# Encoder layer with Strassen products: VectorE takes all subtracts of Down's resident operands, earlier, and block 1's weights' sums are spread

## The chip, the core and the metric

One core of a Trainium2 chip runs the whole kernel as one program. TensorE (PE) multiplies, VectorE (DVE), ScalarE (ACT) and GpSimd (POOL) do everything elementwise, and SyncE (SP) issues the DMAs. The metric is the time of one execution on the device, in microseconds; the times given are medians of several executions.

## The reference

The kernel computes one encoder layer for two batches, 2048 and 1024 positions of width 1024, in float32. The change lies wholly in the second half, the channel mixer:

```python
def _rmsnorm(x, g):
    xf = x.astype(jnp.float32)
    y = xf * lax.rsqrt(jnp.mean(xf * xf, axis=-1, keepdims=True) + EPS)
    return (y * g.astype(jnp.float32)).astype(x.dtype)

def _channel_mixer(h, w_up, conv_w, conv_b, w_down):
    a = h @ w_up                                   # (tokens, 1024) x (1024, 5632)
    ap = jnp.pad(a, ((0, 0), (1, 1), (0, 0)))
    a = ap[:, :-2] * conv_w[0] + ap[:, 1:-1] * conv_w[1] + ap[:, 2:] * conv_w[2] + conv_b
    gate, up = a[..., :D_FF], a[..., D_FF:]        # D_FF = 2816
    return (jax.nn.gelu(gate) * up) @ w_down       # (tokens, 2816) x (2816, 1024)

def _trunk(x, ...):
    m = _token_mixer(_rmsnorm(x, pre_mix_norm[l]), ...)
    x = x + _rmsnorm(m, post_mix_norm[l])
    c = _channel_mixer(_rmsnorm(x, pre_ffn_norm[l]), ...)
    x = x + _rmsnorm(c, post_ffn_norm[l])
```

## The kernel before

**Arithmetic.** Each float32 operand is split in two parts that TensorE multiplies: `h`, a rounded copy made by a ScalarE cast, and `l = x - h`, made by a subtract on VectorE or, for some, on GpSimd. A product is then three matmuls per 128 rows of the inner dimension: h times h, h times l, l times h. On top of this each matrix product of 2x2 blocks is done in the Strassen-Winograd form: seven block products in place of eight, of sums of blocks.

**The two projections.** *Up* (h times w_up) runs in three blocks of 1024 tokens (block 0 to 2), each 22 steps. The right operands of a block, seven operands of four parts (`sox`), stay in SBUF for all its steps; the left operands, seven a step, come from the weights (`a0u` to `a6u` are loaded, then cast and subtracted into `w0u` to `w6u`). A step is seven products `p0u` to `p6u` of 12 matmuls each. Its results are combined by VectorE in PSUM (`vu`, `ru`, `p5u`, ...), go through the convolution's taps (VectorE, line 1153) and the gate: gelu on ScalarE, then GpSimd multiplies 128 x 1024 (`t0u`, line 1190). *Down* multiplies that with w_down in three groups of the inner dimension, q0 (three parts an operand, 9 matmuls a product), q1 and q2 (four parts, 12 matmuls), each 12 steps over the tokens. The resident operands of a group (`sow`, from the loaded `srw`) are 7 x 3 or 7 x 4 tiles of one unit. Here GpSimd forms the four left sums of a step (`s0d` to `s3d`, lines 181 to 184), and VectorE adds the products to the results (`c0d`, `c1d`, ..., line 1307), which wait in DRAM between groups.

**The sums of Down's weights.** Four of the seven right operands of Down are sums of blocks of w_down. They are formed once, while Up's block 1 runs: eleven times `wd_load` (four loads of 256 KB), `wd_sums` (four GpSimd operations 128 x 512, lines 126 to 128 and 694) and `wd_store` (four stores to `wo_d`).

**What sets the order.** `at(slot, order, fn)` enters a function in a table. At the end the table is run through by slot, and within a slot by order (LOAD, PREP, MM, OUT, STORE). Each engine executes its own instructions in that order, and waits by semaphores for the others. A slot holds one product of TensorE in the phases here, a step seven slots. Left operands are prepared three slots ahead of their product in blocks 1 and 2, two in Down. A change from one block or group to the next is `turnover(s, stage, order, lead, span)` (line 251): the 28 parts of the next seven operands are entered from `lead` slots ahead of the first product on, spread over `span` slots; each is loaded three slots before it is cast and subtracted (`Stage.prep`, line 148).

**Storage.** Tiles of 128 x 1024 come from a pool of 43 units, halves of 128 x 512 from a pool of 14, banks of PSUM from eight. A new tile takes the place of an old one once its last reader is done.

Of the kernel before, what the change touches and what calls it, by code (L numbers as in the profile page):

```python
# [15 lines left out]
ALU = mybir.AluOpType  # L16
# [17 lines left out]
def tile_trunk(  # L34
# [6 lines left out]
    nc = tc.nc  # L41
# [5 lines left out]
    def unit(name, dt=F32, shape=(128, 1024)):  # L47
        return U.tile(list(shape), dt, tag="u", name=name)

    def half(name, dt=F32, shape=(128, 512)):  # L50
        return H.tile(list(shape), dt, tag="h", name=name)
# [30 lines left out]
    vec = nc.vector  # L82
# [32 lines left out]
    LOAD, PREP, MM, OUT, STORE = range(5)  # L115

    def at(slot, order, fn, *args):
        events[slot].append((order, len(events[slot]), fn, args))
# [3 lines left out]
    B11, B21, T4, T2, T3, T1, B22 = range(7)  # L122

    def right_sums(t1, b11, b12, b21, b22, last=True):

        nc.gpsimd.tensor_tensor(t1, b12, b11, op=ALU.subtract)
        nc.gpsimd.tensor_tensor(b12, b22, b12, op=ALU.subtract)
        nc.gpsimd.tensor_tensor(b11, b12, b11, op=ALU.add)
        if last:
            nc.gpsimd.tensor_tensor(b21, b11, b21, op=ALU.subtract)  # L130


    class Stage:
# [14 lines left out]
        def prep(self, j, ks=range(4)):  # L148
            for k in ks:
                if k >= self.n:  # L150
                    return
                r = self.raw[j][k]
                t = unit(f"so{self.name}{j}{k}", F32R, (128, 2, 512))
                nc.scalar.copy(t[:, 0], r)
                eng = vec if k % 2 == 0 or self.name == 'x0' and j in (B11, T2) else nc.gpsimd
                eng.tensor_tensor(t[:, 1], r, t[:, 0].bitcast(F32), op=ALU.subtract)  # L156
                self.raw[j][k] = None
                self.op[j] = (self.op[j] or []) + [t]
# [74 lines left out]
    def place(s, step, which=None):  # L233

        step.s0, step.by = (s, 1) if which is None else (s + which, 2)

    def pos(step, k):
        return step.s0 + min(k, 0) + step.by * min(max(k, 0), 6) + max(k - 6, 0)

    def steps(step, ahead=2):  # L240
        at(pos(step, -6), LOAD, step.load)
        at(pos(step, -ahead), PREP - 0.2, step.sums)
        products(step)

    def products(step):
        for i, j in enumerate(step.ORDER):
            at(pos(step, i) - step.LEAD, PREP, step.prep, j)
            at(pos(step, i), MM, step.mm, j)
            at(pos(step, i), OUT, step.post, j)

    def turnover(s, stage, order=tuple(range(7)), lead=6, span=10):

        for n in range(28):
            j, k = order[n // 4], n % 4
            d = s - lead + n * span // 28
            if k % 2 == 0:
                at(d - 3, LOAD, stage.load, j, (k,))
            at(d, PREP + 0.1, stage.prep, j, (k,))
# [329 lines left out]
    for pr in range(12):  # L588
        s = SB + 7 * pr
# [97 lines left out]
            nc.sync.dma_start(bs[q], wd[(ka, kb)[q // 2], :, c : c + 512])  # L687
        raws["wd", i] = bs

    def wd_sums(i):  # L690
        t1 = half(f"wt{i}")
        bs = raws["wd", i]
        right_sums(t1, *bs, False)
        nc.gpsimd.tensor_tensor(bs[2], bs[2], bs[0], op=ALU.subtract)
        bs.append(t1)

    def wd_store(i):
        b11, b12, b21, _, t1 = raws.pop(("wd", i))
# [322 lines left out]
    for i, m in enumerate(mixes):  # L1021
        s = B1 + 4 * i
# [180 lines left out]
    s = B1 + 4 * len(mixes)  # L1203
    for blk in range(3):

        def x_src(j, a, m, dst, blk=blk):
            nc.sync.dma_start(dst[:, :m], xo_d[blk, j, :, a : a + m])

        stage = Stage(f"x{blk}", 4, x_src)
        if blk == 1:  # L1210
            for i in range(NFT // 2):
                at(s + 7 * i + 22, LOAD, wd_load, i)
                at(s + 7 * i + 25, PREP, wd_sums, i)
                at(s + 7 * i + 29, STORE, wd_store, i)
        if blk:
            turnover(s, stage, Up.ORDER, 12, 22)
        else:
            for i, j in enumerate(Up.ORDER):
                d = s + max(2 * i - 3, -2)
                at(d - 1 - (i > 0), LOAD, stage.load, j)  # L1220
                at(d, PREP - 0.3, stage.prep, j)
        for ft in range(NFT):
            u = Up(stage, blk, ft)

            pair = ft < 2 or ft > NFT - 3
            place(s - 7 * (ft % 2) if pair else s, u, ft % 2 if pair else None)
            first = blk == 0 and ft < 2
            if first:
                u.POOL = ()
                at(u.s0 - 2, LOAD, u.load)  # L1230
                at(u.s0 - 2, PREP - 0.2, u.sums)
                products(u)
            elif blk == 0:
                steps(u, 3)
            else:
                for i, j in enumerate(u.ORDER):
                    at(pos(u, i) - 6, LOAD, u.load_left, j)
                products(u)
            if blk == 0:
                at(u.s0 + (4 if pair else 2), STORE, u.sstore)  # L1240
            at(pos(u, 4), OUT + 0.1, u.centre, 1)
            at(pos(u, 4) + 1, OUT + 0.2, u.taps, 1, 0)
            at(pos(u, 4) + 2, OUT + 0.2, u.taps, 1, 1)
            at(pos(u, 6), OUT + 0.1, u.centre, 0)
            at(pos(u, 7), OUT + 0.2, u.taps, 0, 0)
            at(pos(u, 8), OUT + 0.6, u.taps, 0, 1)
            at(pos(u, 10), OUT + 0.3, u.gate)
            at(pos(u, 12), STORE, u.store)
            s += 7
        if blk == 1:  # L1250
            at(s + 5, OUT + 0.5, last_token)
            at(s + 6, STORE, last_token_store)
# [106 lines left out]
    for q in range(3):  # L1359

        def w_src(j, a, m, dst, q=q):
            k0, n = GROUPS[q]
            kk = KPAIRS.index((k0, k0 + n)) + a
            if j in (B11, B21, B22):
                k = k0 + a + (0 if j == B11 else n)
                c = 512 if j == B22 else 0
                src = wd[k : k + m, :, c : c + 512]
            else:
                src = wo_d[(T1, T2, T3, T4).index(j), kk : kk + m]
            nc.sync.dma_start(dst[:, :m], src.rearrange("k p n -> p k n"))  # L1370

        stage = Stage(f"w{q}", GROUPS[q][1], w_src)
        turnover(s, stage, Down.ORDER, *(() if q else (10, 14)))
        if q == 2:
            at(s - 2, LOAD, po_load)
        for tp in range(12):
            d = Down(stage, q, tp)
            place(s, d)
            steps(d, 3)
            if q == 0:  # L1380
                at(s + 8, STORE, d.cstore)
                s += 7
                continue
            at(s - 2, LOAD, d.cload)
            if q == 1:
                at(s + 8, STORE, d.cstore2, 0)
                at(s + 8, STORE, d.cstore2, 1)
            elif tp == 11:
                at(s + 1, LOAD, d.closing_load)
                at(s + 2, OUT + 0.1, d.square, 0, 0)  # L1390
                at(s + 4, OUT + 0.1, d.square, 1, 1)
                at(s + 5, OUT + 0.1, d.square, 0, 1)
                at(s + 6, OUT + 0.1, d.square, 1, 0)
                at(s + 6, OUT + 0.2, d.closing_out)
            else:
                e = 3 if d.closing else 0
                at(s + 10 - e, MM, d.squares)
                at(s + 11 - e, LOAD, d.xload)
                at(s + 11 - e, PREP + 0.5, d.scale)
                at(s + 12 - e, PREP + 0.5, d.yout, 1)  # L1400
                at(s + 14 - e, OUT + 0.3, d.yout, 0)
                at(s + 14 - e, STORE, d.ystore, 1)
                at(s + 15 - e, STORE, d.ystore, 0)
            s += 7
# [121 lines left out]
```

## Time and profile before

| | before |
|---|---|
| median of 3 runs | 2758.53 us (2756.62 to 2758.92) |
| the profiled execution | 2759.55 us |
| its span in the trace | 2757.6 us |
| granted TensorE clock, mean | 0.986 |
| TensorE busy | 2650.9 us, 96% |
| VectorE busy | 2156.4 us, 78% |
| ScalarE busy | 1199.7 us, 44% |
| GpSimd busy | 1172.1 us, 43% |

The span is the time from the first to the last instruction in the trace; it is a little less than the time of the execution. Busy is the sum over an engine's instructions. Since TensorE is busy nearly throughout, the interesting part is the rest of its span: where it waits, and for whom. The page's list of costly groups is a sum over all stages and doesn't tell this; the table of stretches and the timelines do. Matmul records are pipelined and their ends modelled, so a count of matmuls in a stretch says more than the busy time.

### The profile page before, as it was taken

Reading aid. Unit: us, or ns where it says so; the run is one execution under the profiler, and the core shown is the slowest. Engines: PE = TensorE matmul, PEld = TensorE weight load, DVE = VectorE, ACT = ScalarE, POOL = GpSimd, SP = SyncE. Lnnn points to the kernel's source line nnn. Section 1 sums busy time; section 2 is a strip of 40 time slices with the busy share of each in tenths; the row PEclk is TensorE's granted clock in tenths of the full one; section 3 lists DMA queues with packets and bytes.
Section 4 is the critical chain, followed back from the end, with each engine's and each line's share of the span. In section 5 each row is a group of like instructions: output and inputs, shape, how many; then the busy total and the mean of one; then the engine's idle time right before and its main releaser. Section 6 shows DMA issues by size and latency. Waiting matters only on the chain.

```text
span 2757.6 us, 35060 instructions
## 1 busy us (share of the span) xinstructions
PE 2650.9 (96%) x11930; PEld 2164.6 (78%) x11930; DVE 2156.4 (78%) x3282; ACT 1199.7 (44%) x2261; POOL 1172.1 (43%) x772
## 2 busy tenths in 40 slices
PE   8899999999889999999999998999998999999998
PEld 7788877887768888877777886888886877887886
DVE  6777756678888788888888888888887567668887
ACT  5445524555544444454333444444444352224333
POOL 3644221235655556643444233222124344326666
PEclk9999999999999999999999999999999999999999
DMA  9223375658934445564665364343353475456665
GB/s 350 104 84 115 122 276 203 228 175 282 334 134 155 155 155 180 180 209 148 217 220 198 129 221 123 107 138 124 117 181 129 131 234 167 160 184 229 206 222 198
DMA packets 323923, 498.08 MB, mean 181 GB/s; under 512 B 27232, under 2 KB 176224, under 8 KB 323744
## 3 DMA queue, kind: packets, MB, share of 16 engines
q1 hardware_dynamic: 323744, 495.85, 54.3%
q8 instruction: 93, 1.52, 0.2%
q14 instruction: 86, 0.70, 0.1%
HBM read 337.42 MB, written 158.35 MB: 180 GB/s over the span
## 4 chain that ended last, share of the span: by engine, by line
PE 43%; DVE 7%; issue 3%; ACT 1%; DMA 1%; POOL 0%; SPq 0%; DVEq 0%; ACTq 0%; POOLq 0%
PE p0d L203 12%; PE p5u L203 4%; PE p4u L203 4%; PE p2u L203 4%; PE p3u L203 4%; PE p6d L203 3%; PE p0u L203 3%; PE p1d L203 3%; PE p5d L203 3%; PE p1u L203 3%; PE p6u L203 2%; DVE sow L156 1%; DVE w3u L101 1%; DVE t1u L1153 1%; DVE t0u L1153 1%
## 5 line engine op out<-in xcount | busy, mean ns | idle before, releaser
L1190 POOL TENSOR_TENSOR t0u<-t0u,t1u 128x1024 f32<-128x1024 f32 x66 | 177.3, 2688 | 424.7 <-ACT t0u L1189 267.2
L203 PE MATMUL p0u<-sox,w0u 128*128 128x512 f32 x792 | 194.6, 394 | 11.7 <-DVE w0u L101 11.6
L203 PE MATMUL p1u<-sox,w1u 128*128 128x512 f32 x792 | 194.3, 392 | 6.8 <-DVE w1u L101 6.6
L203 PE MATMUL p3u<-sox,w3u 128*128 128x512 f32 x792 | 195.2, 393 | 5.7 <-DVE w3u L101 4.9
L203 PE MATMUL p5u<-sox,w5u 128*128 128x512 f32 x792 | 194.0, 392 | 6.2 <-DVE w5u L101 6.2
L203 PE MATMUL p4u<-sox,w4u 128*128 128x512 f32 x792 | 192.7, 392 | 5.5 <-POOL w4u L101 5.0
L203 PE MATMUL p2u<-sox,w2u 128*128 128x512 f32 x792 | 191.9, 392 | 5.1 <-DVE w2u L101 5.1
L203 PE MATMUL p6u<-sox,w6u 128*128 128x512 f32 x792 | 191.1, 391 | 1.2 <-DVE w6u L101 1.2
L203 PEld LDWEIGHTS p0u<-sox,w0u 128*128 128x128 f32 x792 | 149.1, 189 | 47.3 <-DVE w0u L101 16.3
L1141 ACT ACTIVATE t1u<-p2u,cbt,cwt 128x512 f32<-128x512 f32 x66 | 51.5, 780 | 301.1 <-DVE p2u L1129 293.3
L203 PEld LDWEIGHTS p1u<-sox,w1u 128*128 128x128 f32 x792 | 147.2, 188 | 44.3 <-DVE w1u L101 13.3
L203 PEld LDWEIGHTS p3u<-sox,w3u 128*128 128x128 f32 x792 | 146.8, 188 | 43.9 <-DVE w3u L101 11.9
L203 PEld LDWEIGHTS p5u<-sox,w5u 128*128 128x128 f32 x792 | 146.6, 188 | 43.9 <-DVE w5u L101 12.8
L203 PEld LDWEIGHTS p4u<-sox,w4u 128*128 128x128 f32 x792 | 147.1, 188 | 42.5 <-POOL w4u L101 8.5
L203 PEld LDWEIGHTS p2u<-sox,w2u 128*128 128x128 f32 x792 | 149.8, 189 | 37.2 <-DVE w2u L101 5.9
L203 PEld LDWEIGHTS p6u<-sox,w6u 128*128 128x128 f32 x792 | 148.9, 188 | 33.9 <-DVE w6u L101 2.8
L1141 ACT ACTIVATE t0u<-p1u,cbt,cwt 128x512 f32<-128x512 f32 x66 | 51.5, 780 | 256.8 <-DVE p1u L1135 256.8
L1189 ACT ACTIVATE t0u<-t0u 128x1024 f32<-128x1024 f32 x66 | 70.1, 1062 | 171.2 <-DVE t0u L1153 139.3
L181 POOL TENSOR_TENSOR s0d<-ra1d 128x512 f32<-128x512 f32 (+1 forms) x36 | 50.2, 1396 | 204.1 <-DMA ra1d<-g_d 190.1
L93 POOL TENSOR_SCALAR r_v<-ss 128x2 f32<-128x2 f32 (+1 forms) x38 | 15.9, 417 | 261.4 <-ACT scr L894 156.7
L101 POOL TENSOR_TENSOR w4u<-a4u,w4u 128x512 fp32r<-128x512 f32 x44 | 61.3, 1395 | 143.6 <-ACT w4u L100 119.9
L1153 DVE SCALAR_TENSOR_TENSOR t0u<-p6u,cwt,t0u 128x511 f32<-128x511 f32 (+4 forms) x220 | 111.9, 534 | 7.1 <-ACT t0u L1141 2.0
(348 smaller groups left out, 7040.5 us busy)
## 6 DMA issues: line engine op xcount, KB each, us to landing
g_d<-t0u SPq DMA_DIRECT2D x66, 512.0 KB, 2.9
srx<-xo_d SPq DMA_DIRECT2D x42, 512.0 KB, 6.5
xT<-xT SPq DMA_DIRECT2D x24, 512.0 KB, 8.1
xc<-xc SPq DMA_DIRECT2D x24, 512.0 KB, 5.3
zz<-z_d SPq DMA_DIRECT2D x48, 256.0 KB, 5.8
xr<-x_po SPq DMA_DIRECT2D x24, 512.0 KB, 4.9
xo_d<-hT SPq DMA_DIRECT2D x48, 256.0 KB, 3.6
ra0d<-g_d SPq DMA_DIRECT2D x24, 512.0 KB, 4.6
```

What stands on the lines that cost most here:

```text
L93: nc.gpsimd.tensor_scalar(v, ss, 1.0 / n, EPS, op0=ALU.mult, op1=ALU.add)
L101: (eng or vec).tensor_tensor(l, src, h.bitcast(F32), op=ALU.subtract)
L156: eng.tensor_tensor(t[:, 1], r, t[:, 0].bitcast(F32), op=ALU.subtract)
L181: nc.gpsimd.tensor_tensor(s1, a21, a22, op=ALU.add)
L203: nc.tensor.matmul(ps, lhsT=w[:, a, k], rhs=op[k][:, b], start=k == 0 and a + b == 0 and not chained, stop=k == n - 1 and a == 1, skip_gro ...
L1141: nc.scalar.activation(t[:, i], p, AF.Identity, bias=cbt[:, ti : ti + 1], scale=cwt[:, ti, 1:2])
L1153: vec.scalar_tensor_tensor(d, a, w, d, op0=ALU.mult, op1=ALU.add)
L1189: nc.scalar.activation(ga, ga, AF.Gelu_apprx_tanh)
L1190: nc.gpsimd.tensor_tensor(ga, ga, self.t[1], op=ALU.mult)
```

## The change

Three edits, all in the channel mixer.

1. `Stage.prep`: for stages with a name in `w` (Down's three groups), VectorE does the subtract of every part. Before, GpSimd did it for the odd parts.
2. `wd_sums` becomes four calls, each of one GpSimd operation. The group of sums i begins at slot 10 + 12 i of block 1 instead of 22 + 7 i: loads there, the sums 3, 5, 7 and 9 slots on, the stores 11 slots on.
3. `turnover` of Down: lead and span are (14, 18) for q0, (16, 20) for q1 and (7, 11) for q2; before (10, 14), (6, 10) and (6, 10).

```diff
--- before.py
+++ after.py
@@ -152,7 +152,7 @@
                 r = self.raw[j][k]
                 t = unit(f"so{self.name}{j}{k}", F32R, (128, 2, 512))
                 nc.scalar.copy(t[:, 0], r)
-                eng = vec if k % 2 == 0 or self.name == 'x0' and j in (B11, T2) else nc.gpsimd
+                eng = vec if k % 2 == 0 or self.name[0] == 'w' or self.name == 'x0' and j in (B11, T2) else nc.gpsimd
                 eng.tensor_tensor(t[:, 1], r, t[:, 0].bitcast(F32), op=ALU.subtract)
                 self.raw[j][k] = None
                 self.op[j] = (self.op[j] or []) + [t]
@@ -687,12 +687,17 @@
             nc.sync.dma_start(bs[q], wd[(ka, kb)[q // 2], :, c : c + 512])
         raws["wd", i] = bs
 
-    def wd_sums(i):
-        t1 = half(f"wt{i}")
+    def wd_sums(i, n):
+
         bs = raws["wd", i]
-        right_sums(t1, *bs, False)
-        nc.gpsimd.tensor_tensor(bs[2], bs[2], bs[0], op=ALU.subtract)
-        bs.append(t1)
+        if n == 0:
+            bs.append(half(f"wt{i}"))
+        b11, b12, b21, b22, t1 = bs
+        out, x, y, op = (
+            (t1, b12, b11, ALU.subtract), (b12, b22, b12, ALU.subtract),
+            (b11, b12, b11, ALU.add), (b21, b21, b11, ALU.subtract),
+        )[n]
+        nc.gpsimd.tensor_tensor(out, x, y, op=op)
 
     def wd_store(i):
         b11, b12, b21, _, t1 = raws.pop(("wd", i))
@@ -1209,9 +1214,11 @@
         stage = Stage(f"x{blk}", 4, x_src)
         if blk == 1:
             for i in range(NFT // 2):
-                at(s + 7 * i + 22, LOAD, wd_load, i)
-                at(s + 7 * i + 25, PREP, wd_sums, i)
-                at(s + 7 * i + 29, STORE, wd_store, i)
+                d = s + 10 + 12 * i
+                at(d, LOAD, wd_load, i)
+                for n in range(4):
+                    at(d + 3 + 2 * n, PREP, wd_sums, i, n)
+                at(d + 11, STORE, wd_store, i)
         if blk:
             turnover(s, stage, Up.ORDER, 12, 22)
         else:
@@ -1370,7 +1377,7 @@
             nc.sync.dma_start(dst[:, :m], src.rearrange("k p n -> p k n"))
 
         stage = Stage(f"w{q}", GROUPS[q][1], w_src)
-        turnover(s, stage, Down.ORDER, *(() if q else (10, 14)))
+        turnover(s, stage, Down.ORDER, *((14, 18), (16, 20), (7, 11))[q])
         if q == 2:
             at(s - 2, LOAD, po_load)
         for tp in range(12):
```

Line numbers behind the second edit grow by 5 to 7: the gate's product t0u is on line 1195 after the change, the adds of Down on 1314. TensorE's order stays as it was.

GpSimd in block 1, where the weights' sums begin; before: in `w4u1_3` the 1 is the block and the 3 the step, `t0u` is the gate's product, `wd` and `wt` are the weights' tiles.

```order
L1190 TENSOR_TENSOR t0u1_1_11144<-t0u1_1_11144,t1u1_1_11046 128x1024
L101 TENSOR_TENSOR w4u1_3_11296<-a4u1_3_11225,w4u1_3_11296 128x512
L1190 TENSOR_TENSOR t0u1_2_11313<-t0u1_2_11313,t1u1_2_11266 128x1024
L126 TENSOR_TENSOR wt0_11420<-wd01_11345,wd00_11344 128x512
L127 TENSOR_TENSOR wd01_11345<-wd03_11347,wd01_11345 128x512
L128 TENSOR_TENSOR wd00_11344<-wd01_11345,wd00_11344 128x512
L694 TENSOR_TENSOR wd02_11346<-wd02_11346,wd00_11344 128x512
L101 TENSOR_TENSOR w4u1_4_11471<-a4u1_4_11396,w4u1_4_11471 128x512
L1190 TENSOR_TENSOR t0u1_3_11488<-t0u1_3_11488,t1u1_3_11442 128x1024
```

The same steps after the change:

```order
L1195 TENSOR_TENSOR t0u1_0_11130<-t0u1_0_11130,t1u1_0_11021 128x1024
L700 TENSOR_TENSOR wd00_11053<-wd01_11054,wd00_11053 128x512
L1195 TENSOR_TENSOR t0u1_1_11154<-t0u1_1_11154,t1u1_1_11046 128x1024
L700 TENSOR_TENSOR wd02_11055<-wd02_11055,wd00_11053 128x512
L101 TENSOR_TENSOR w4u1_3_11309<-a4u1_3_11236,w4u1_3_11309 128x512
L1195 TENSOR_TENSOR t0u1_2_11326<-t0u1_2_11326,t1u1_2_11278 128x1024
L700 TENSOR_TENSOR wt1_11437<-wd11_11362,wd10_11361 128x512
L700 TENSOR_TENSOR wd11_11362<-wd13_11364,wd11_11362 128x512
L101 TENSOR_TENSOR w4u1_4_11486<-a4u1_4_11413,w4u1_4_11486 128x512
L700 TENSOR_TENSOR wd10_11361<-wd11_11362,wd10_11361 128x512
L700 TENSOR_TENSOR wd12_11363<-wd12_11363,wd10_11361 128x512
L1195 TENSOR_TENSOR t0u1_3_11503<-t0u1_3_11503,t1u1_3_11456 128x1024
```

The four sums of a group, which stood in one row between t0u and w4u, now stand one or two at a time on either side of w4u, and the first group is through when step 3's gate is reached.

VectorE ahead of the first left operand of q1, `w0d1_0`; before: `sow1jk` is part k of q1's operand j, `w4d0_11` a left operand of q0's last step.

```order
L156 TENSOR_TENSOR sow112_19813<-srw112_19729,sow112_19813 128x512
L156 TENSOR_TENSOR sow130_19819<-srw130_19731,sow130_19819 128x512
L1307 TENSOR_TENSOR c1d0_11_19804<-c1d0_11_19804,p5d0_11_19822 128x512
L101 TENSOR_TENSOR w2d0_11_19843<-ra1d0_11_19623,w2d0_11_19843 128x384
L156 TENSOR_TENSOR sow132_19849<-srw132_19748,sow132_19849 128x512
L1309 TENSOR_TENSOR c3d0_11_19864<-c3d0_11_19864,p5d0_11_19822 128x512
L101 TENSOR_TENSOR w0d1_0_19875<-ra0d1_0_19750,w0d1_0_19875 128x512
L156 TENSOR_TENSOR sow150_19878<-srw150_19781,sow150_19878 128x512
```

The same place after the change:

```order
L156 TENSOR_TENSOR sow141_19852<-srw140_19761,sow141_19852 128x512
L156 TENSOR_TENSOR sow142_19855<-srw142_19780,sow142_19855 128x512
L1314 TENSOR_TENSOR c1d0_11_19845<-c1d0_11_19845,p5d0_11_19858 128x512
L101 TENSOR_TENSOR w2d0_11_19877<-ra1d0_11_19648,w2d0_11_19877 128x384
L156 TENSOR_TENSOR sow143_19880<-srw142_19780,sow143_19880 128x512
L1316 TENSOR_TENSOR c3d0_11_19892<-c3d0_11_19892,p5d0_11_19858 128x512
L101 TENSOR_TENSOR w0d1_0_19901<-ra0d1_0_19800,w0d1_0_19901 128x512
L156 TENSOR_TENSOR sow160_19904<-srw160_19828,sow160_19904 128x512
```

Before, 6 of VectorE's 14 subtracts stand ahead of w0d1_0, the even parts only; after, 20 of 28, odd parts between the even ones, and they begin in q0's step 10.

## Rows read from the trace of the kernel before

**Rows 1.** The page: span, and each engine's busy time.
```profile
span 2757.6 us, 35060 instructions
PE 2650.9 (96%) x11930; PEld 2164.6 (78%) x11930; DVE 2156.4 (78%) x3282; ACT 1199.7 (44%) x2261; POOL 1172.1 (43%) x772
```

**Rows 2.** Stretches: length; PE, PEld, DVE, ACT, POOL busy (count); PEclk, DMA share, GB/s.
```profile
1290.00:1400.00 110.00, 105.95 (x448) 82.16 (x447) 96.17 (x154) 42.06 (x69) 54.65 (x33) 1.00 0.67 216
...
1511.00:1603.00 92.00, 92.00 (x408) 76.17 (x407) 79.01 (x146) 40.12 (x66) 21.20 (x10) 1.00 0.39 129
...
2030.00:2110.00 80.00, 71.06 (x296) 56.66 (x295) 72.37 (x134) 39.29 (x69) 32.25 (x21) 0.96 0.48 156
2110.00:2240.00 130.00, 130.00 (x575) 107.63 (x574) 65.74 (x101) 48.31 (x102) 44.48 (x40) 1.00 0.43 135
2240.00:2310.00 70.00, 61.20 (x250) 48.53 (x249) 55.44 (x59) 32.21 (x62) 41.94 (x26) 0.93 0.75 248
2310.00:2470.00 160.00, 160.00 (x708) 132.48 (x707) 101.08 (x128) 37.35 (x60) 52.14 (x36) 1.00 0.50 165
2470.00:2560.00 90.00, 84.30 (x355) 68.27 (x354) 72.18 (x79) 33.35 (x59) 46.81 (x30) 0.96 0.66 222
```

**Rows 3.** Waits of TensorE, 1290 to 1500: total us, times, longest.
```profile
PE p3u L203 <- DVE w3u L101: 4.9, 10, 0.5
PE p1u L203 <- DVE w1u L101: 3.2, 10, 0.3
```

**Rows 4.** Timeline of GpSimd, one step of block 1: start, length, instruction [idle before].
```profile
1448.85 2.40 POOL L1190 TENSOR_TENSOR t0u<-t0u,t1u 128x1024 f32<-128x1024 f32 x1 [10.45 <-ACT t0u L1189]
1451.19 1.75 POOL L126 TENSOR_TENSOR wt<-wd,wd 128x512 f32<-128x512 f32 x1
...
1456.19 1.30 POOL L694 TENSOR_TENSOR wd<-wd,wd 128x512 f32<-128x512 f32 x1
...
1469.62 2.40 POOL L1190 TENSOR_TENSOR t0u<-t0u,t1u 128x1024 f32<-128x1024 f32 x1 [10.43 <-ACT t0u L1189]
```

**Rows 5.** Timeline of VectorE, the same step.
```profile
1448.43 0.69 DVE L1122 TENSOR_TENSOR ru<-vu,p4u 128x512 f32<-128x512 f32 x1
1449.03 2.76 DVE L101 TENSOR_TENSOR w1u<-a1u,w1u 128x512 fp32r<-128x512 f32 x1
...
1452.91 0.68 DVE L101 TENSOR_TENSOR w0u<-a0u,w0u 128x512 fp32r<-128x512 f32 x1
...
1456.28 1.75 DVE L101 TENSOR_TENSOR w3u<-a3u,w3u 128x512 fp32r<-128x512 f32 x1 [2.08 <-ACT w3u L100]
```

**Rows 6.** Timelines of GpSimd and VectorE in a step of block 1 without sums.
```profile
1566.44 2.95 POOL L1190 TENSOR_TENSOR t0u<-t0u,t1u 128x1024 f32<-128x1024 f32 x1 [10.36 <-ACT t0u L1189]
...
1584.85 2.94 POOL L1190 TENSOR_TENSOR t0u<-t0u,t1u 128x1024 f32<-128x1024 f32 x1 [10.37 <-ACT t0u L1189]
...
1566.45 0.69 DVE L101 TENSOR_TENSOR w1u<-a1u,w1u 128x512 fp32r<-128x512 f32 x1
...
1568.24 1.70 DVE L101 TENSOR_TENSOR w0u<-a0u,w0u 128x512 fp32r<-128x512 f32 x1
...
1572.58 0.69 DVE L101 TENSOR_TENSOR w3u<-a3u,w3u 128x512 fp32r<-128x512 f32 x1 [2.03 <-ACT w3u L100]
```

**Rows 7.** The tile sow: casts and subtracts, ns min/median/max, first and last start.
```profile
L154 ACT CAST sow<-srw x77: 613/620/635, 2054.6 to 2523.0; 128x512 fp32r<-128x512 f32 x77
L156 DVE TENSOR_TENSOR sow<-srw,sow x42: 677/1760/2900, 2057.2 to 2528.9; 128x512 fp32r<-128x512 f32 x42
L156 POOL TENSOR_TENSOR sow<-srw,sow x35: 1273/1719/1792, 2056.7 to 2523.7; 128x512 fp32r<-128x512 f32 x35
```

**Rows 8.** Waits of TensorE, longest of 2030-2110, 2240-2310, 2470-2560.
```profile
PE p0d L203 <- DVE w0d L101: 3.9, 1, 3.9
PE p0d L203 <- DVE c0d L1307: 4.9, 1, 4.9
PE p0d L203 <- ACT sow L154: 3.1, 1, 3.1
```

## The prediction

> **What bounds the kernel now.** I read the page first: TensorE is busy 96% of the span, so all that any reordering can win is about 106 us of its idle time [rows 1]. The second view, a table of stretches, shows where that lies. In the undisturbed Down stretch 2310 to 2470, TensorE runs 708 matmuls in 160 us, 0.226 us each. Taking each stretch's length less its matmuls at 0.226 gives what it loses: 8.8 us in 1290-1400 (448), nothing in 1511-1603 (408), 13.1 in 2030-2110 (296), 13.5 in 2240-2310 (250), 9.8 in 2470-2560 (355) [rows 2]. The first is block 1 of Up while GpSimd forms the weights' sums; the last three are the starts of Down's groups q0, q1 and q2. The change touches these four places and no other.
>
> The third view, the waits, says who is late. In block 1 it is VectorE's w1u and w3u, ten times each within 1290-1500 [rows 3]. At q0 it is w0d, at q1 the add c0d, both VectorE; at q2 a cast sow of ScalarE [rows 8].
>
> The timelines say why. One step of block 1 lasts from one product t0u on GpSimd (1448.85) to the next (1469.62), 20.77 us [rows 4]; a step's 84 matmuls need 84 x 0.226 = 18.98. GpSimd is not full, but VectorE's subtracts stretch beside it: w1u, started 0.18 us after t0u, lasts 2.76 us, until 0.54 after t0u's end; w3u, started 0.09 us after the sum of line 694, lasts 1.75. The operation ru, with one operand in PSUM, keeps 0.69 [rows 5]. Without sums the same chain has a period of 18.41 (1566.44 to 1584.85), less than TensorE needs: w1u starts with t0u and takes 0.69, w0u takes the wait instead (1.70), w3u is 0.69 [rows 6]. So the weights' sums turn a VectorE chain of 18.41 into one of 20.77.
>
> **Part 1, the sums in block 1.** Nothing is added: 44 sums remain, four per group, eleven groups; loads (four of 256 KB a group) and stores (four) move with them in SP's queue. They stood as four in a row in each of eleven steps, between t0u and w4u. Now they stand two slots apart over slots 13 to 139 of the block's 154, so 44 in about 18.3 steps, 2.4 a step, mostly one or two behind t0u and the rest behind w4u.
> - What is lost now: 1.79 us x 11 steps = 19.7 by the periods; 8.8 in 110 us is 1.66 a step, 18.2. I use 18.
> - Where it comes from [rows 5, 6]: w1u +2.07, w0u -1.02, w3u +1.06, 2.11 of the 2.36. With at most two sums behind t0u (2.40 + 1.75 + 1.75 = 5.9 us [rows 4]) GpSimd has finished before w3u starts, 6.14 us after t0u (1572.58 - 1566.44): the 1.06 goes. The w1u part is a race with t0u, lost by 0.18 us now and won without sums.
> - If w1u wins again the period is 18.4 to 18.9, TensorE bounds it at 18.98, and 18 us are saved. If it still loses, the period is 18.41 + 2.07 - 1.02 = 19.46, 0.48 over, x 18.3 = 8.8 us lost, 9 saved. At the worst end each sum holds up one subtract by the 1.06 of w3u (rival A), 18 lost in place of saved.
> - The first loads now stand in SP's queue among the loads of the block's first steps, and the last sums run up to block 2's turnover; I charge 1 to 2 us for these two together.
> Value: -14, ends -18 and +18.
>
> Sentences on the chip's notes: in rows 5 only subtracts with both operands in SBUF stretch, and to the end of a GpSimd operation. The Trainium skill ("SBUF — State Buffer", "Who interferes with whom") says so: a VectorE instruction with two SBUF inputs and a GpSimd one that reads SBUF exclude each other for a whole instruction, whichever came first. The trace agrees (2.76 against 0.69). By that rule spreading sums wins nothing in itself, since each of 44 may meet a subtract of its own: that is rival A.
>
> **Part 2, 35 subtracts from GpSimd to VectorE.** GpSimd does 35 of the operands' subtracts (sow) at 1.72 us, VectorE 42 with a median of 1.76 and a least of 0.68 [rows 7]; the least is what it costs with GpSimd idle, and consecutive ones start 0.60 apart (1448.43 to 1449.03 [rows 5]). With none left on GpSimd, its remaining work there is t0u and the four left sums of each step, so I price VectorE's subtract at 0.60; ends 0.60 and 1.76. The last is what it costs today beside GpSimd's own, the cause that goes, so I stand near the first. The issue slots differ by group.
>
> q1 (lead 6 slots and span 10 become 16 and 20; a slot of q0 is 9 x 0.226 = 2.03 us). Before: 14 x 1.72 = 24.1 us of subtracts in 10 slots, 20.3 us. In q0's steady stretch VectorE is busy 65.74 of 130, 51% [rows 2], so 10.0 us were free: 14 short, and 13.5 are lost. That the two agree is why I trust the sum. After: 28 x 0.60 = 16.8 in 20 slots, 40.7 us, with 20 free. Nothing is short but single collisions with step sums; I leave 2. Saved 11.5, ends 4 and 13.
>
> q2 (6, 10 become 7, 11; a slot is 12 x 0.226 = 2.71). Before: 14 x 1.76 = 24.6 in 27.1 us, of which VectorE has 101.08/160 taken [rows 2], 10.0 free: 14.6 short, 9.8 lost. After: 16.8 in 29.8, 11.0 free: 5.8 short, by the same 9.8/14.6 that is 3.9 lost. Saved 6, ends 0 and 9.
>
> q0 (10, 14 become 14, 18). Three operands a product, so VectorE gets 7 more. Ahead of w0d, for which TensorE waits 3.9 us [rows 8], 15 subtracts stand instead of 8: +7 x 0.60 = 4.2 at one end. At the other, GpSimd's 7 no longer hold subtracts up, at most 7 x 1.07 = 7.5: -3.3. VectorE is about 86% busy there (79.01 of 92 in the like stretch [rows 2]), so starting four slots earlier finds only 4 x 2.71 x 0.14 = 1.5 us. Value +1, near the middle.
>
> Behind this, SP's 42 loads of operands start 4, 10 and 1 slots sooner, past the loads of left operands of the steps then running; those are issued six slots ahead of use, 12 us or more, and I charge nothing; if that cover is gone, some 2 us at q1. ScalarE's casts move with them: 0.62 us each [rows 7] x 28 = 17 in 41 us at q1, beside its 48.31 of 130 [rows 2], fits.
>
> **Sum.** -14 + 1 - 11.5 - 6 = -30.5 on the profiled execution's 2759.55 (span 2757.6 [rows 1] and 1.95 around it): 2729.05. The median of the runs is 1.0 lower, so 2728.
>
> **Rivals.**
> A, sums still collide, one by one. For: the stretch is per operation, and w3u's 1.06 came from one sum. Against: VectorE works from PSUM for half the step. 44 x 1.06 = 46.6 over 18.3 steps is 2.55 a step: a period of 20.96, 1.98 over, 36 lost against 18. With part 2 as forecast: 2728 + 32 = 2760, no change.
> B, the turnovers stay, under another name: operands cannot be resident sooner. For: the pool has 43 units; q0's 21 and q1's 28 are 49 before anything else, so the last casts wait for q0's last step to release its operands, and ScalarE's casts of left operands are queued behind them; at q2 the cast is the late one already [rows 8]. Against: the casts stand close to where the units come free. Each of the last step's seven products then waits for a cast and a subtract, 0.62 + 0.69 = 1.3: 9 of q1's 13.5 stay, and 8 of q2's 9.8: 2728 + 7 + 4 = 2739.
> C, slower: the subtract stays long on VectorE although GpSimd's are gone (step sums and t0u hold it, or the stretch is not GpSimd's). At 1.76 each: q1 28 x 1.76 = 49.3 less 20 free, 29 lost; q2 38 short x 0.67 = 25.7; q0 21 x 1.76 = 37 less 6.8, 30. That is 85 against 36 now, +49, with part 1's -14 that is +35: 2793. It decides from about 1.25 us a subtract: 28 x 1.25 - 20 = 15 at q1, 16 at q2, 19 at q0, 50 in all, 14 more than now, which uses up part 1. Against: the 0.68 in rows 7 and the 0.69 in rows 6.
>
> **How the numbers follow.** Forecast 0.62, its own range 2713 to 2741 (part 1 at -18 or -9, q0 -3 to +4, q1 and q2 at their ends in part). B 0.17, A 0.14, C 0.07. Within 0.2% is 5.5 us, about what a measurement of this kernel tells from no change. Faster: all of the forecast, B, and a third of A, 0.84; same: most of the rest of A, 0.08; slower: C and a little of A, 0.08. The range that holds 8 in 10 takes the forecast and B with part of A: 2713 to 2748.
>
> **What would show it.** Right: GpSimd's t0u in block 1 repeat every 18.9 to 19.1 us and w3u is 0.69; TensorE's waits for w1u and w3u are gone; the 77 sow on VectorE have a median near 0.7; 2240-2310 and 2470-2560 lose under 3 and 5 us. Wrong: a period of 19.4 (the race lost) or 20.9 (A); waits of TensorE for ScalarE's casts at q1 (B); a median of sow over 1.25 (C); a q0 that loses over 17.

## The result, and the profile after

The changed kernel takes 2726.36 us, median of 4 runs (2724.16 to 2728.02), beside 2757.9 for the kernel before (4 runs, 2756.62 to 2758.92). The ratio is 0.9885, 95% interval 0.9868 to 0.9903: 31.5 us faster, forecast 30.5. The profiled execution took 2726.56 us, its span is 2724.5.

TensorE issues its products in one order in all kernels here, so the two traces can be laid side by side: for each change from one product to the next, its start before less its start after. That difference grows or shrinks only where something was gained or lost. From the timelines of TensorE:

| place | forecast | gained in the traces |
|---|---|---|
| block 1, while the weights' sums are formed | 14 | 17.4 |
| start of q0 | -1 | -3.8 |
| start of q1 | 11.5 | 12.9 |
| start of q2 | 6 | 5.2 |

About 1 us more comes in at block 2's start, and 0.5 goes again in its last step. The rest of the difference in span (33.1), 0.9, lies ahead of block 1, where no edit acts and where the traces of the kernels below differ from the one before by -1.8 to 3.3 us.

The same table of stretches, of the changed kernel (length; busy time and count of PE, PEld, DVE, ACT, POOL; PEclk, DMA share, GB/s); it answers to [rows 2]. Places are up to 33 us earlier in time, so only the first line covers just the same work:

```profile
1290.00:1400.00 110.00, 110.00 (x487) 91.09 (x486) 94.60 (x174) 47.70 (x78) 45.01 (x26) 1.00 0.57 185
...
2030.00:2110.00 80.00, 66.81 (x277) 52.32 (x276) 67.35 (x118) 37.06 (x69) 29.36 (x21) 0.96 0.42 137
...
2240.00:2310.00 70.00, 69.61 (x307) 57.32 (x306) 53.68 (x69) 26.01 (x47) 30.41 (x20) 1.00 0.69 232
...
2470.00:2560.00 90.00, 87.36 (x377) 71.58 (x377) 77.15 (x93) 35.25 (x62) 48.36 (x31) 0.98 0.69 231
```

In block 1 TensorE does 487 matmuls in 110 us instead of 448, 0.226 us each: nothing is lost. q1's stretch loses 70 - 307 x 0.226 = 0.6 instead of 13.5, q2's 4.8 instead of 9.8, q0's 17.4 instead of 13.1.

The waits of TensorE at q0 (2030 to 2110), and at q2 (2470 to 2560); q1 keeps one of 0.4. They answer to [rows 8], and the waits of [rows 3] are gone:

```profile
PE p0d L203 <- DVE w0d L101: 6.3, 1, 6.3
PE p0d L203 <- ACT c0d L1310: 2.0, 1, 2.0
PE p5d L203 <- DVE w5d L101: 1.8, 1, 1.8
PE p6d L203 <- DVE w6d L101: 1.5, 1, 1.5
PE p0d L203 <- DVE w4d L101: 1.3, 1, 1.3
...
PE p0d L203 <- DVE c1d L1314: 2.2, 1, 2.2
PE p0d L203 <- ACT w5d L100: 0.4, 1, 0.4
```

At q0 VectorE is late for as many left operands as before, with w6d in the place of w2d, and w0d by 6.3 instead of 3.9. The others at q0 before:

```profile
PE p5d L203 <- DVE w5d L101: 1.3, 1, 1.3
PE p0d L203 <- DVE w4d L101: 1.3, 1, 1.3
PE p0d L203 <- DVE w2d L101: 0.8, 1, 0.8
```

Not all that is lost is waiting. At q1 before, TensorE's waits add up to 8.9 of the 13.5 us. Behind the longest one its next twelve matmuls take 4.79 us (2281.14 to 2285.93), where twelve undisturbed ones take 12 x 0.226 = 2.7 (TensorE's timeline, then a stretch as in [rows 2]):

```profile
2281.14 4.95 PE L203 MATMUL p0d<-sow,w3d 128*128 128x512 f32 x12 [4.88 <-DVE c0d L1307]
2285.93 2.89 PE L203 MATMUL p5d<-sow,w5d 128*128 128x512 f32 x12
...
2280.00:2290.00 10.00, 8.10 (x26) 6.28 (x27) 10.00 (x10) 1.76 (x3) 9.92 (x7) 0.73 0.34 106
```

The granted clock of that stretch is 0.73: after the idle time TensorE ran part of it at the lower of its two levels (1.2 GHz), its matmuls 0.43 us apart. After the change the whole of q1's stretch is at 1.00, so part of what q1 gains is clock and not waiting.

One step of block 1 on GpSimd and VectorE (start, length); it answers to [rows 4, 5]:

```profile
1375.60 2.95 POOL L1195 TENSOR_TENSOR t0u<-t0u,t1u 128x1024 f32<-128x1024 f32 x1 [10.41 <-ACT t0u L1194]
1378.51 1.74 POOL L700 TENSOR_TENSOR wt<-wd,wd 128x512 f32<-128x512 f32 x1
...
1394.01 2.96 POOL L1195 TENSOR_TENSOR t0u<-t0u,t1u 128x1024 f32<-128x1024 f32 x1 [7.79 <-ACT t0u L1194]
...
1375.01 0.68 DVE L1127 TENSOR_TENSOR ru<-vu,p4u 128x512 f32<-128x512 f32 x1
1375.61 0.68 DVE L101 TENSOR_TENSOR w1u<-a1u,w1u 128x512 fp32r<-128x512 f32 x1
...
1377.41 1.69 DVE L101 TENSOR_TENSOR w0u<-a0u,w0u 128x512 fp32r<-128x512 f32 x1
...
1381.72 0.69 DVE L101 TENSOR_TENSOR w3u<-a3u,w3u 128x512 fp32r<-128x512 f32 x1 [2.02 <-ACT w3u L100]
```

t0u repeats after 18.41 us while VectorE catches up, after 19.04 from about 1431 on, where TensorE sets the pace. w1u starts 0.01 us after t0u and isn't held up; w3u starts when GpSimd is idle.

The subtracts of the operands, all on VectorE now (ns min/median/max), to be read beside [rows 7]:

```profile
L156 DVE TENSOR_TENSOR sow<-srw,sow x77: 677/683/2895, 2029.7 to 2496.1; 128x512 fp32r<-128x512 f32 x77
```

The median is what an undisturbed one takes, but the maximum says that some are still held up. The next part shows how much that is.

### The profile page after: what moved, and what is told of

Read it like the earlier page. It is cut to its first block, busy times and chain, and to the rows that moved or that the text cites. A ratio compares the mean times of both kernels' runs of the same rounds, so it can differ in the third digit from the quotient of the medians.

```text
span 2724.5 us, 35039 instructions
## 1 busy us (share of the span) xinstructions
PE 2634.1 (97%) x11930; PEld 2163.6 (79%) x11930; DVE 2125.3 (78%) x3317; ACT 1199.9 (44%) x2261; POOL 1116.1 (41%) x737
## 5 line engine op out<-in xcount | busy, mean ns | idle before, releaser
L1195 POOL TENSOR_TENSOR t0u<-t0u,t1u 128x1024 f32<-128x1024 f32 x66 | 183.7, 2785 | 414.4 <-ACT t0u L1194 251.3
```

The costliest lines, as they stand in the source:

```text
L1195: nc.gpsimd.tensor_tensor(ga, ga, self.t[1], op=ALU.mult)
```

## Experiments

The table has each run's median, the ratio to the kernel before measured beside it, and what the place-by-place comparison with the trace before gives (us gained). The places are from one execution each; what the spans differ by beyond them lies mostly ahead of block 1 and at block 2's start.

| run | median us | ratio (95%) | block 1 | q0 | q1 | q2 |
|---|---|---|---|---|---|---|
| the change | 2726.36 | 0.9885 (0.9868 to 0.9903) | 17.4 | -3.8 | 12.9 | 5.2 |
| sums only | 2738.99 | 0.993 (0.9915 to 0.9944) | 17.4 | 0.1 | 0.0 | 0.6 |
| VectorE only | 2761.4 | 1.0009 (0.9999 to 1.0018) | 0.0 | -3.2 | 0.0 | -0.3 |
| leads only | 2747.8 | 0.9961 (0.9946 to 0.9976) | 0.0 | 0.2 | 10.0 | 0.4 |
| q0 as before | 2721.03 | 0.9862 (0.9847 to 0.9877) | 17.4 | 0.0 | 12.9 | 6.3 |
| sums two and two | 2734.46 | 0.9913 (0.9898 to 0.9928) | 6.6 | -4.0 | 12.4 | 6.2 |
| four behind w4u | 2735.13 | 0.9912 (0.9896 to 0.9929) | 8.0 | -4.2 | 12.9 | 0.7 |
| q0 odd on GpSimd | 2719.8 | 0.986 (0.9845 to 0.9875) | 17.3 | 0.3 | 12.9 | 5.2 |
| q2 earlier | 2727.4 | 0.9885 (0.987 to 0.99) | 17.4 | -3.9 | 12.9 | 4.7 |
| 16 halves | 2746.36 | 0.9954 (0.9938 to 0.9971) | 12.6 | -1.5 | 0.0 | -0.2 |
| row every 12 | 2727.53 | 0.9891 (0.9877 to 0.9906) | 17.4 | -4.6 | 12.4 | 5.2 |
| q0 two on GpSimd | 2722.59 | 0.9875 (0.9861 to 0.989) | 17.3 | -1.1 | 12.9 | 5.2 |
| q2 old lead | 2725.71 | 0.9881 (0.9864 to 0.9897) | 17.4 | 0.3 | 12.9 | -0.9 |

**Each part alone.** The kernel before with the second edit of the change alone (sums only):

```diff
...
-                at(s + 7 * i + 25, PREP, wd_sums, i)
...
+                d = s + 10 + 12 * i
...
+                    at(d + 3 + 2 * n, PREP, wd_sums, i, n)
...
```

> The kernel before with the weights' sums spread and nothing else. Theory (the parts act at their own places and add): the whole gain of block 1, 17.6 us by the two traces, so about 2740, ratio 0.9936; t0u every 18.4 to 19.0 us, w1u 0.69 and w3u 0.69; the starts of q0, q1 and q2 lose 13.1, 13.5 and 9.8 as before. Rival (block 1's gain needs VectorE and GpSimd to be relieved elsewhere too, or is taken back at block 2's start): 2748 or more.

2739.0 and 17.4 in block 1: the theory. The sums act alone and nothing is taken back.

With the first edit alone (VectorE only):

```diff
-                eng = vec if k % 2 == 0 or self.name == 'x0' and j in (B11, T2) else nc.gpsimd
+                eng = vec if k % 2 == 0 or self.name[0] == 'w' or self.name == 'x0' and j in (B11, T2) else nc.gpsimd
```

> The kernel before with the 35 subtracts moved to VectorE, leads and sums as before. Theory (VectorE's work against its free time): q1 16.8 us of subtracts against 10.0 free in 10 slots, 6.8 short, saves 6.7; q2 6.8 short x 0.67 = 4.6, saves 5; q0 loses 1 to 3: about 2748, ratio 0.996. Rival 1 (the gain at q1 and q2 is the engine's, the lead is idle): q1 saves 12.9, q2 5: 2743. Rival 2 (it is the lead's, the engine is idle): q1 and q2 save nothing, q0 loses 2: 2760.

2761.4: my theory fell, rival 2 stands. Moving the subtracts gains nothing at q1 and q2 and costs 3.2 at q0. GpSimd and VectorE of this run at q1:

```profile
2256.26 1.29 POOL L181 TENSOR_TENSOR s0d<-ra1d 128x512 f32<-128x512 f32 x1 [19.71 <-ACT c0d L1303]
2257.63 1.50 POOL L182 TENSOR_TENSOR s1d<-s0d,ra0d 128x512 f32<-128x512 f32 x1
2259.09 1.74 POOL L183 TENSOR_TENSOR s2d<-ra0d,ra1d 128x512 f32<-128x512 f32 x1
2260.79 1.73 POOL L184 TENSOR_TENSOR s3d<-ra0d,s1d 128x512 f32<-128x512 f32 x1
...
2257.89 5.18 DVE L156 TENSOR_TENSOR sow<-srw,sow 128x512 fp32r<-128x512 f32 x3
2262.99 0.68 DVE L1307 TENSOR_TENSOR c0d<-c0d,p1d 128x512 f32<-128x512 f32 x1
2263.59 0.55 DVE L101 TENSOR_TENSOR w4d<-s2d,w4d 128x384 fp32r<-128x384 f32 x1
2264.06 1.88 DVE L156 TENSOR_TENSOR sow<-srw,sow 128x512 fp32r<-128x512 f32 x3
```

Three subtracts take 1.88 us while GpSimd is idle and 5.18 beside its step sums, one GpSimd operation each. VectorE's sow over q1, before and here (count, busy us, mean ns):

```profile
L156 DVE TENSOR_TENSOR sow<-srw,sow 128x512 fp32r<-128x512 f32 x14 | 23.1, 1663 | 0.3 <-ACT sow L154 0.3
...
L156 DVE TENSOR_TENSOR sow<-srw,sow 128x512 fp32r<-128x512 f32 x28 | 24.2, 917 | 0.0
```

With the leads alone it is 15.7 us for 14, after the change 23.4 for 28. So, at the old lead, 14 more subtracts cost VectorE what the GpSimd ones had cost it in being held up: its total is about the same.

With the third edit alone (leads only):

```diff
-        turnover(s, stage, Down.ORDER, *(() if q else (10, 14)))
+        turnover(s, stage, Down.ORDER, *((14, 18), (16, 20), (7, 11))[q])
```

> The kernel before with the three new leads and spans, the odd subtracts still on GpSimd, sums as before. Theory: at q1 14 x 1.72 = 24.1 us against 20 free in 20 slots, 4.1 short, saves 9.4; q2 13.6 short x 0.67 = 9.1, saves 0.7; q0 -1 to +2: about 2748.5, ratio 0.9963. Rival 1 (the engine's gain): 2758. Rival 2 (the lead's): q1 saves 12.9, q2 5: 2741.

2747.8, q1 10.0 and q2 0.4: the theory, to 0.6 us. Most of q1's gain is the lead's; the engine adds 2.9 on top of it, and at q2 neither alone gives anything while both together give 5.2.

**q0.** The changed kernel with q0 wholly as before (odd subtracts on GpSimd, (10, 14)):

```diff
...
-self.name[0] == 'w'
+self.name in ('w1', 'w2')
...
-        turnover(s, stage, Down.ORDER, *((14, 18), (16, 20), (7, 11))[q])
+        turnover(s, stage, Down.ORDER, *((10, 14), (16, 20), (7, 11))[q])
```

> The changed kernel with q0 as before: its odd subtracts on GpSimd, lead 10 and span 14. Theory (q0 is where the change loses: 15 subtracts ahead of w0d in place of 8): q0 loses 13.1 instead of 16.6, so about 3.5 us less than the changed kernel, 2723, ratio 0.9873; w0d is waited for 3.9 us. Rival (q0's loss only moves: q1's casts find their units later or VectorE is later into q0): same as the changed kernel, 2726, ratio 0.9885.

2721.0, 5.3 below the changed kernel: 3.8 of it at q0 and 1.1 at q2 by the traces. The loss at q0 is the change's, and doesn't move on. With the odd subtracts on GpSimd, but the new lead (q0 odd on GpSimd):

```diff
...
-self.name[0] == 'w'
+self.name in ('w1', 'w2')
...
```

> The changed kernel with q0's odd subtracts back on GpSimd but q0's new lead and span (14, 18). Theory (the engine loses at q0, the lead does nothing there): q0 as before, 2721 as with q0 wholly as before. Rival (the earlier begin loses, since the casts and subtracts stand among block 2's last pair): as the changed kernel, 2726.

2719.8: q0's loss comes from the engine, not from the lead. Its median is 6.6 us below the change's; of what the two traces differ by, 4.1 us lie at q0 and 2.4 ahead of block 1, where no edit acts. From q0 wholly as before (2716.83 to 2721.94) these runs (2718.92 to 2722.76) can't be told apart. w0d is still waited for longer than before:

```profile
PE p0d L203 <- DVE w0d L101: 5.4, 1, 5.4
```

Going from q0 as before by way of this kernel to the changed one, w0d's wait grows by 1.5 with the new lead and by 0.9 with the engine. With two parts of three on GpSimd (q0 two on GpSimd):

```diff
...
-eng = vec if k % 2 == 0 or self.name[0] == 'w' or
+eng = vec if (k == 0 if self.name == 'w0' else k % 2 == 0 or self.name[0] == 'w') or
...
```

> The changed kernel with two of the three parts of each of q0's operands on GpSimd, 14 subtracts, lead 14 and span 18. Theory (at q0 VectorE's work ahead of w0d sets the loss, and GpSimd is idle for 13 us and 24 us there): 7 subtracts fewer than with the odd ones alone on GpSimd, 7 x 0.60 = 4.2 us, less what they hold up: q0 loses 10 to 13, 2717 to 2720. Rival (each GpSimd subtract costs VectorE as much as its own): 2723 or more.

2722.6, the rival: w0d is waited for 2.6 us instead of 5.4 with the odd ones there, but w4d 3.5 instead of 1.3. With seven more subtracts on GpSimd q0 loses 1.1 instead of gaining 0.3: by the waits, what is spared at w0d is lost again at the operands behind it.

**Where the sums stand.** Two kernels, each the changed one with its sums in eleven steps again. The first, two behind t0u and two behind w4u (two and two):

```diff
-                d = s + 10 + 12 * i
+                d = s + 7 * i + 22
...
-                    at(d + 3 + 2 * n, PREP, wd_sums, i, n)
-                at(d + 11, STORE, wd_store, i)
+                    at(d + (3, 3, 8, 8)[n], PREP, wd_sums, i, n)
+                at(d + 10, STORE, wd_store, i)
```

> The changed kernel, but the 44 sums again in eleven steps, four a step: two behind t0u and two behind w4u. Theory (it is the place that counts: GpSimd must be done when w3u starts, and then w1u wins its race with t0u): block 1 as in the changed kernel, 17.4 us saved, about 2726, w1u and w3u 0.69. Rival (density counts, each sum costs VectorE about the same 0.5 us wherever it stands): a period near 20.5 again, 15 to 18 us lost, about 2743.

The second, four behind w4u:

```diff
-                d = s + 10 + 12 * i
+                d = s + 7 * i + 25
...
-                    at(d + 3 + 2 * n, PREP, wd_sums, i, n)
-                at(d + 11, STORE, wd_store, i)
+                    at(d + 5, PREP, wd_sums, i, n)
+                at(d + 9, STORE, wd_store, i)
```

> The changed kernel, but the 44 sums in eleven steps, four in a row behind w4u instead of between t0u and w4u. Theory (only a subtract that starts while GpSimd runs is held up): w3u free, but the row of four, 8.0 to 13.3 us after t0u, now meets w5u, which starts 11.9 us after t0u: one subtract held up by about 1.07, a period near 19.5, 5 to 7 us lost in eleven steps, about 2732. Rival 1 (only w1u and w3u matter): 2726. Rival 2 (a row of four costs 2.36 wherever it stands): 2743.

2734.5 and 2735.1: neither theory nor rival in either. The timeline of the first shows why (GpSimd, then VectorE):

```profile
1424.00 2.40 POOL L1195 TENSOR_TENSOR t0u<-t0u,t1u 128x1024 f32<-128x1024 f32 x1 [7.80 <-ACT t0u L1194]
1429.43 1.29 POOL L700 TENSOR_TENSOR wt<-wd,wd 128x512 f32<-128x512 f32 x1 [3.03 <-DMA a4u<-ws_d]
1430.80 1.29 POOL L700 TENSOR_TENSOR wd<-wd,wd 128x512 f32<-128x512 f32 x1
...
1423.69 0.69 DVE L1127 TENSOR_TENSOR ru<-vu,p4u 128x512 f32<-128x512 f32 x1 [0.20 <-PE p2u L203]
1424.29 2.65 DVE L101 TENSOR_TENSOR w1u<-a1u,w1u 128x512 fp32r<-128x512 f32 x1
...
1431.37 1.27 DVE L101 TENSOR_TENSOR w3u<-a3u,w3u 128x512 fp32r<-128x512 f32 x1 [2.02 <-ACT w3u L100]
```

The sums keep their order but not their time: the first two wait 3.03 us for a DMA and start 5.4 us after t0u, where w3u meets one of them (1.27 us). And ru waits 0.20 us, with the result that w1u starts 0.29 us after t0u and is held up. In the second kernel w3u is free, but w5u meets the row, as the theory had it (1.12 us on average from 1300 to 1500), and w1u is held up in some steps (1.40 on average). Both kernels form a group every seven slots, as before, and keep its halves two or three slots longer. That gave a new theory: it is the pool of 14 halves that makes ru late. The kernel before, with nothing of the change but two halves more (16 halves):

```diff
-    U = ctx.enter_context(tc.tile_pool(name="u", bufs=43))
-    H = ctx.enter_context(tc.tile_pool(name="h", bufs=14))
+    U = ctx.enter_context(tc.tile_pool(name="u", bufs=42))
+    H = ctx.enter_context(tc.tile_pool(name="h", bufs=16))
```

> The kernel before with two more halves (16) for one unit less (42); nothing of the change. New theory (the rows of four cost block 1 in two ways: they meet w3u, and their halves, up to 9 of 14 held at a time, make ru wait 0.18 us, by which w1u starts behind t0u and loses 2.07): with 16 halves ru doesn't wait, w1u takes 0.69 and w0u 1.70; w3u stays 1.75; a period of 18.41 + 1.06 = 19.5, 0.5 over 18.98, so 5 us lost in block 1 in place of 18: 2746 if the unit less costs nothing elsewhere. Rival (w1u loses because the chain is late from w3u, halves don't matter): block 1 as before, 2759, w1u 2.76.

2746.4, as the new theory had it. The rows of four still stand between t0u and w4u (GpSimd, then VectorE):

```profile
1441.77 2.96 POOL L1190 TENSOR_TENSOR t0u<-t0u,t1u 128x1024 f32<-128x1024 f32 x1 [9.18 <-ACT t0u L1189]
...
1461.29 2.95 POOL L1190 TENSOR_TENSOR t0u<-t0u,t1u 128x1024 f32<-128x1024 f32 x1 [9.17 <-ACT t0u L1189]
...
1440.57 0.68 DVE L101 TENSOR_TENSOR w6u<-a6u,w6u 128x512 fp32r<-128x512 f32 x1
1441.17 0.68 DVE L1122 TENSOR_TENSOR ru<-vu,p4u 128x512 f32<-128x512 f32 x1
1441.77 0.69 DVE L101 TENSOR_TENSOR w1u<-a1u,w1u 128x512 fp32r<-128x512 f32 x1
...
1443.57 1.70 DVE L101 TENSOR_TENSOR w0u<-a0u,w0u 128x512 fp32r<-128x512 f32 x1
...
1447.90 1.81 DVE L101 TENSOR_TENSOR w3u<-a3u,w3u 128x512 fp32r<-128x512 f32 x1 [2.02 <-ACT w3u L100]
```

A period of 19.52 instead of 20.77: ru no longer waits, w1u wins its race, and w3u still meets a sum. Of block 1's 17.4 us, 12.6 come with the halves alone; 4.8 are left for w3u. At q0 1.5 are lost, perhaps by the unit less.

The programs built from the kernels say what ru waits for. With 14 halves, in the kernel before and in two and two, ru takes the place of a6u in steps 4 to 13, and those are the ten steps in which w1u is held up. The last reader of a6u is w6u, the subtract just ahead of ru on VectorE; in the step of [rows 5]:

```profile
1447.65 0.68 DVE L101 TENSOR_TENSOR w6u<-a6u,w6u 128x512 fp32r<-128x512 f32 x1
```

So ru starts there at 1448.43, 0.10 us after w6u's end. With 16 halves ru takes the place of a5u, free long before, and starts 0.08 us ahead of w6u's end. The p2u that the timeline of two and two names isn't what ru waited for.

The changed kernel with the four sums of a group in one slot, still a group every 12 slots (row every 12):

```diff
-                    at(d + 3 + 2 * n, PREP, wd_sums, i, n)
+                    at(d + 3, PREP, wd_sums, i, n)
```

> The changed kernel with the four sums of a group in one slot again, but still a group every 12 slots. New theory (halves and the number a step decide, not the distance of two slots): w1u keeps winning its race; a row meets w3u or w5u in about every second step, 1.06 us, which the 0.57 us of slack in each step nearly hides: 0 to 4 us lost, 2726 to 2730. Rival (spreading one per two slots is what pays): w1u loses to t0u behind each row as well, 18.41 + 2.1 in eleven steps of 18, 10 us or more lost, 2736.

2727.5, 17.4 in block 1: one sum per two slots is not what pays. VectorE's subtracts there, 1300 to 1500 (count, busy us, mean ns):

```profile
L101 DVE TENSOR_TENSOR w0u<-a0u,w0u 128x512 fp32r<-128x512 f32 x11 | 17.6, 1604 | 0.0
L101 DVE TENSOR_TENSOR w3u<-a3u,w3u 128x512 fp32r<-128x512 f32 x11 | 9.8, 895 | 22.5 <-ACT w3u L100 22.5
L101 DVE TENSOR_TENSOR w1u<-a1u,w1u 128x512 fp32r<-128x512 f32 x11 | 9.6, 871 | 0.0
```

w3u still meets a row now and then (mean 895 ns, against 1755 before), and w1u loses its race in one of the eleven steps (mean 871); so few such steps fit into the 0.57 us that each step has to spare.

**q2.** The changed kernel with (10, 14) at q2:

```diff
-        turnover(s, stage, Down.ORDER, *((14, 18), (16, 20), (7, 11))[q])
+        turnover(s, stage, Down.ORDER, *((14, 18), (16, 20), (10, 14))[q])
```

> The changed kernel with (10, 14) for q2 in place of (7, 11). Theory (free time of VectorE, three slots more give 3 x 2.71 x 0.37 = 3 us): q2 loses 1.7 instead of 4.7, about 2723. Rival (units: q1's 28 operands and q2's 28 are 56 for 43, so the casts before slot -7 wait for the last step of q1 and hold ScalarE up): q2 loses more than now, 2730 or above, with TensorE waiting for casts of ScalarE.

2727.4, neither: the wait for c1d is all but gone (2.2 to 0.2), and one of 2.6 us for a cast sow on ScalarE has come in its place. The casts wait, as the rival has it, but TensorE loses by it no more than the lead gives. Last, the kernel with q0's odd subtracts on GpSimd, with q2 at its old (6, 10):

```diff
-        turnover(s, stage, Down.ORDER, *((14, 18), (16, 20), (7, 11))[q])
+        turnover(s, stage, Down.ORDER, *((14, 18), (16, 20), (6, 10))[q])
```

> The kernel with q0's odd subtracts on GpSimd (2719.8), but q2 at its old lead and span, (6, 10). Theory (at q2 the two edits work only together: with VectorE doing all 28 its own work no longer fits 10 slots, with one slot more it does): q2 loses 9.8 as before, about 2725, TensorE waiting for casts of ScalarE. Rival (the engine's move is what gains at q2, and the run with it alone lost it only to its state behind q1): q2 loses about 5, 2720.

2725.7: q2 loses all it had gained. TensorE at q2, and ScalarE in front of it:

```profile
PE p0d L203 <- ACT w1d L100: 4.1, 1, 4.1
PE p0d L203 <- DVE c0d L1314: 2.0, 1, 2.0
...
2490.49 0.62 ACT L100 CAST w0d<-ra0d 128x512 fp32r<-128x512 f32 x1 [2.85 <-DVE sow L156]
2493.83 0.62 ACT L100 CAST w1d<-ra0d 128x512 fp32r<-128x512 f32 x1 [2.73 <-DVE sow L156]
```

ScalarE's casts of left operands wait for VectorE's subtracts, and TensorE for them. One slot of lead decides that, 6.1 us in all. The programs say for which units: at the old lead, with all 28 on VectorE, w0d and w1d of q2's second step take the places of two raw tiles (srw) that VectorE's subtracts read last. With (7, 11) w0d takes one that a store has freed, and only w1d takes such a place. The lead (7, 11) stands close to the edge: the profiled execution of the kernel with four sums behind w4u, 5 us above its median, shows the same 4 us wait for w1d, and gains 0.7 at q2 instead of 5.2.

## Why the prediction was right, point by point

- **Where the time was.** The four places and the sizes of their losses held; outside them no more than about 1 us changed at a place. The forecast of 30.5 against 31.5 is in part luck: block 1 and q1 gave 3.4 and 1.4 more, q0 and q2 took 2.8 and 0.8.
- **Part 1, -14; measured -17.4.** The mechanism was right: w3u meets a sum, w1u loses a race by 0.18 us, and without sums TensorE sets the pace. The charge of 1 to 2 us for loads and late stores and the allowance for a lost race were not needed. What I had not named is why w1u lost: not the sums on GpSimd, but their tiles, which leave ru the place of a6u. Two halves more in the old kernel win 12.6 of the 17.4.
- **Part 2, a VectorE subtract at 0.60.** This step failed in size. 28 subtracts at q1 took 23.4 us, not 16.8, since GpSimd's step sums hold VectorE up as GpSimd's own subtracts had. I had counted those sums only as part of the 51% in the steady stretch, and nothing for what they do to the subtracts added there. The move by itself gains nothing, where by my sum it would have gained 6.7 at q1 and 5 at q2.
- **q1, -11.5; measured -12.9.** Right, through the lead: 10.0 of it without the move. The comparison of work with free time forecast those 10.0 to 0.6, but this is weak support: the same sum missed the move alone by 6.7. That 14 short and 13.5 lost agreed was luck in part: it set GpSimd's 1.72 a subtract against VectorE's free time, and only 8.9 of the 13.5 are waits, the rest in good part matmuls at the lower clock behind them, which the sum doesn't hold.
- **q2, -6; measured -5.2.** The number held, its working did not: neither edit alone gives it, and one slot of lead is worth 6.1 there once all 28 stand on VectorE, since at the old lead ScalarE's casts of left operands wait for units that VectorE's subtracts free. A free-time sum has no such edge in it.
- **q0, +1; measured +3.8.** Inside its ends (-3.3 to +4.2), at the upper one. The relief was overrated: with the leads new in both, moving the seven subtracts costs 3.8 + 0.3 = 4.1. That this is about 7 x 0.60 is chance: w0d's wait, which the sum was about, differs between these two by 0.9 only (5.4 to 6.3), and the seven cost VectorE 5.9 us (sow 12.1 us for 14, 18.0 for 21).
- **The rivals.** A (each sum meets a subtract) did not happen: only w0u is held up in a step, by t0u, as without sums. B (units) didn't show at q1; at q2 the wait for a cast that comes with the longer lead (10, 14) fits it. C asked for a median above 1.25 us; it is 0.68.
- **The rule of the Trainium skill** that a VectorE instruction with two SBUF inputs and a GpSimd one that reads SBUF exclude each other for a whole instruction, whichever came first (the Trainium skill, "SBUF — State Buffer", "Who interferes with whom") fits: 1.88 against 5.18 us for three subtracts, and the race, where 0.18 us late costs w1u 2.07. That w1u wins with a start 0.01 us behind t0u's says that the profile's starts don't show who came first as closely as that. The rule speaks for looking at who starts first, which is what decided 12.6 us of block 1.

What stays open: whether the change of units at q2, a jump from one slot to the next, is worth all of the 6.1 us; no run changes the units there alone.

## What to carry to other kernels

When two engines hold each other up, moving work between them can leave the total as it was: add up the busy time of the engine that is late, with and without the move, before counting the relief. Look at what the moved work occupies, not only where it runs: here two more tiles in a pool gave 12.6 of the 17.4 us that the new order gave in block 1. And give work that must be done by a given moment a longer lead before giving it another engine; where the lead is close to an edge, a few slots more are cheap (three at q2 cost 0.5 us).

## What the runs showed of the hardware

A race of 0.2 us decides 2 us: w1u at 0.01 us after t0u (1375.61 against 1375.60) takes 0.68 us, at 0.18 us after it 2.76. The loser pays unequally: GpSimd's t0u takes 2.95 us instead of 2.40 when w1u goes first, 0.55 more; VectorE loses 2.07 when t0u does. Behind a row of GpSimd operations each VectorE subtract waits for one of them only (three in 5.18 us), not for the row.
